# Gate and up of six ffn chunks as 2 by 2 blocks with seven block products, in a two-layer mixer network on one core

## The chip, the cores and the metric

The kernel runs on one core of one Trainium2 chip. TensorE multiplies, VectorE and ScalarE do the elementwise work, GpSimd and SyncE mostly issue transfers. The metric is the device time in microseconds, the median of the runs shown. Traces of profiled executions show where it goes.

## The reference

Each of two layers applies, to 256 tokens of width 1024, a SwiGLU ffn, a mixer, cross attention to 256 memory tokens, and a second ffn; a layer-norm stands behind each. All is float32.

```python
D_FF = 2816
def swiglu(x, w_gate, w_up, w_down):
    return (jax.nn.silu(x @ w_gate) * (x @ w_up)) @ w_down
...
    for l in range(DEPTH):
        h = layer_norm(ALPHA * h + 0.5 * swiglu(h, ffn1_gate[l], ffn1_up[l], ffn1_down[l]),
                       ln_g[l, 0], ln_b[l, 0])
        ...
        h = layer_norm(ALPHA * h + mix, ln_g[l, 1], ln_b[l, 1])
        h = layer_norm(ALPHA * h + cross_attn(h, mem, ca_q[l], ca_k[l], ca_v[l], ca_o[l]),
                       ln_g[l, 2], ln_b[l, 2])
        h = layer_norm(ALPHA * h + 0.5 * swiglu(h, ffn2_gate[l], ffn2_up[l], ffn2_down[l]),
                       ln_g[l, 3], ln_b[l, 3])
```

## The kernel before

The activations are two tiles `h[0]` and `h[1]` of 128 tokens x 1024. Every float32 product is made of three products of shorter numbers: an operand is split into a high half (`hi`, a cast on ScalarE) and a low half (`lo`, the value less its high half, on VectorE), and `mm_rows` adds hi x hi, hi x lo and lo x hi. `split` (lines 60 to 62) issues the cast (L61) and the subtraction (L62). Weights are split on the chip: `load` fetches 1 MB into a `raw` tile (three of them) and splits it in two pieces of 128x1024 into tiles `whi` and `wlo` (eight of each). A 128x512 product with 128 rows of the contraction is three matmuls.

An ffn (line 380) walks over its 2816 hidden columns in five chunks of 512 and one of 256. For a chunk, `all_products` multiplies the transposed activations `xTh`, `xTl` with gate and with up: 2 token tiles x 8 slices of the contraction x 3 = 48 matmuls each, 96 for both, into PSUM tiles `acc`. ScalarE takes silu of the gate product into `sg` (L406), VectorE multiplies it with up's (`gated`, L410). `turn` transposes the result: four transfers deal it to the tile `dealt`, VectorE's 32x32 block transpose writes `square` (L422), and a split makes `ah` and `al`. With these the rows of `down` are multiplied into four sums `dn` (`ys[i][m]`: token tile i, half m of the columns), which are kept over the whole ffn. The chunk's down products follow one chunk behind.

`finish` (line 292) closes an ffn and the other blocks: `tail` multiplies the last three down pieces, for h0's two sums and then h1's, and VectorE adds each sum to `h` (L320), takes its statistics (L322, L324), adds epsilon (L326), waits for GpSimd's power (L327), and normalises in two steps of two halves each (L330, L334). Then `h[0]` goes to the next block by eight transposes on TensorE (L170) or, behind an ffn1, by way of `deal`: a copy, four transfers, two block transposes on VectorE (L546). `h[1]` follows by TensorE when the next block calls `pend`.

Most of the program is ordered by a scheduler of the framework, which follows its own estimates of when operands are there. Stretches under `manual_schedule` keep the order in which they are written, for the engines named. Each engine runs its own instructions in order.

## Time and profile before

| | |
|---|---|
| runs, us | 1099.81, 1097.89, 1098.06; median 1098.06 |
| span of the profiled execution | 1094.9 us |
| TensorE, mean granted clock | 0.998 |
| TensorE matmuls, busy | 1079.6 us (99%) |
| VectorE, ScalarE, GpSimd busy | 836.3 us, 585.0 us, 61.0 us |
| transfers | 232.90 MB, mean 213 GB/s |

The profile gives no time of its own for the profiled execution but the span, from its first instruction to its last; the runs' median is 3.2 us above it. In the views, PE is TensorE, PEld its weight load, DVE VectorE, ACT ScalarE, POOL GpSimd, SP SyncE. L62 is line 62 of the kernel. A group's row gives its count, the busy time and the mean of one in ns, then the idle time of the engine ahead of it and what ended it. The busy time of neighbouring matmuls overlaps, so their pitch is read from the chain. Between engines the time of an ffn can be read in its stages: chunk after chunk TensorE takes 20.72 us for gate and up and 10.36 us for down.

### The profile page before, as it was taken

What the parts mean: (1) busy time and instruction counts of PE and PEld (TensorE: products, weight loads), DVE (VectorE), ACT (ScalarE), POOL (GpSimd) and SP (SyncE); (2) the same over time, 40 slices, a digit from 0 to 9 for tenths busy, and PEclk for the clock granted to TensorE, in tenths of its full rate; (3) what the DMA queues carried; (4) which work ended last, traced back from release to release, by engine and by line L of the source; (5) the groups of instructions that cost most, each with busy time, mean ns of one, the idle gap of its engine ahead of it and who ended that gap; (6) DMA issues with size and microseconds to landing.
All of it is one profiled execution on the core that took longest, in us unless ns stands there. A gap on an engine that the chain in (4) does not pass through costs nothing.

```text
span 1094.9 us, 15563 instructions
## 1 busy us (share of the span) xinstructions
PE 1079.6 (99%) x6035; PEld 952.6 (87%) x6035; DVE 836.3 (76%) x1075; ACT 585.0 (53%) x811; POOL 61.0 (6%) x113
## 2 busy tenths in 40 slices
PE   9999999999999999999999999999999999999997
PEld 7888888889898888888888888888898988888886
DVE  6679678898889877666687655798988888766665
...
GB/s 326 302 285 226 212 215 170 244 180 164 185 273 176 141 293 217 237 214 217 154 266 265 218 216 206 231 143 261 183 135 217 229 208 163 259 242 211 219 167 38
DMA packets 123818, 232.90 MB, mean 213 GB/s; under 512 B 6432, under 2 KB 46656, under 8 KB 118624
## 3 DMA queue, kind: packets, MB, share of 16 engines
...
HBM read 216.15 MB, written 1.05 MB: 198 GB/s over the span
## 4 chain that ended last, share of the span: by engine, by line
PE 90%; DVE 7%; ACT 2%; issue 1%; DMA 0%; DVEq 0%; ACTq 0%
PE acc L106 60%; PE dn L106 27%; DVE wlo L62 2%; PE acc L170 1%; DVE square L971 1%; PE dn L766 1%; ACT xT L61 0%; DVE qTl L62 0%; DVE h L334 0%; ACT whi L61 0%; DMA h<-in_x_dram 0%; DVE h L330 0%; PE dn L825 0%; DVE xT L62 0%; DVE st L322 0%
## 5 line engine op out<-in xcount | busy, mean ns | idle before, releaser
L62 DVE TENSOR_TENSOR wlo<-raw,whi 128x1024 fp32r<-128x1024 f32 (+1 forms) x396 | 474.1, 1213 | 181.4 <-ACT whi L61 170.6
L61 ACT CAST whi<-raw 128x1024 fp32r<-128x1024 f32 (+1 forms) x396 | 402.5, 1040 | 312.4 <-PE dn L106 117.3
L106 PE MATMUL acc<-whi,xT 128*128 128x512 f32 x1312 | 395.0, 380 | 0.0
L106 PEld LDWEIGHTS acc<-whi,xT 128*128 128x128 f32 x1312 | 247.8, 189 | 35.2
L106 PE MATMUL acc<-wlo,xT 128*128 128x512 f32 x656 | 248.6, 379 | 0.0
L106 PE MATMUL acc<-xT,whi 128*128 128x512 f32 x576 | 142.6, 382 | 4.0 <-DVE xT L62 4.0
L106 PEld LDWEIGHTS acc<-wlo,xT 128*128 128x128 f32 x656 | 124.0, 189 | 17.5
L106 PE MATMUL dn<-whi,ah 128*128 128x512 f32 x346 | 131.3, 379 | 0.0
L106 PE MATMUL dn<-wlo,ah 128*128 128x512 f32 x346 | 131.1, 379 | 0.0
L106 PE MATMUL dn<-whi,al 128*128 128x512 f32 x346 | 131.1, 379 | 0.0
L106 PEld LDWEIGHTS acc<-xT,whi 128*128 128x128 f32 x576 | 103.8, 190 | 16.3 <-ACT whi L61 4.6
L106 PE MATMUL dn<-whi,xT 128*128 128x512 f32 x288 | 88.8, 383 | 0.0
L106 PEld LDWEIGHTS acc<-xT,wlo 128*128 128x128 f32 x576 | 75.6, 191 | 4.3 <-DVE wlo L62 0.4
L106 PE MATMUL acc<-xT,wlo 128*128 128x256 f32 x576 | 76.4, 275 | 0.0
L106 PEld LDWEIGHTS dn<-wlo,ah 128*128 128x128 f32 x346 | 65.4, 189 | 9.3
L106 PEld LDWEIGHTS dn<-whi,al 128*128 128x128 f32 x346 | 65.4, 189 | 9.3
L106 PEld LDWEIGHTS dn<-whi,ah 128*128 128x128 f32 x346 | 65.4, 189 | 9.2
L422 DVE STREAM_TRANSPOSE square<-dealt 128x512 f32<-128x512 f32 x40 | 63.8, 1658 | 0.8 <-DMA dealt<-sg 0.7
L327 POOL TENSOR_TENSOR rs<-rs,nhalf 128x1 f32<-128x1 f32 x16 | 14.9, 929 | 867.3 <-DVE rs L326 859.8
L106 PEld LDWEIGHTS dn<-whi,xT 128*128 128x128 f32 x288 | 54.4, 190 | 8.5 <-DVE xT L62 1.1
L106 PE MATMUL dn<-wlo,xT 128*128 128x512 f32 x144 | 54.7, 380 | 0.0
L320 DVE SCALAR_TENSOR_TENSOR h<-h,dn 128x512 f32<-128x512 f32 x31 | 21.2, 684 | 31.4 <-PE dn L106 31.4
...
## 6 DMA issues: line engine op xcount, KB each, us to landing
raw<-in_ffn_up_dram SPq DMA_DIRECT2D x44, 1024.0 KB, 4.9
raw<-in_ffn_down_dram SPq DMA_DIRECT2D x44, 1024.0 KB, 5.1
raw<-in_ffn_gate_dram SPq DMA_DIRECT2D x42, 1024.0 KB, 5.0
raw<-in_w_in_dram SPq DMA_DIRECT2D x24, 1024.0 KB, 4.9
...
raw<-in_ca_k_dram SPq DMA_DIRECT2D x8, 1024.0 KB, 5.0
raw<-in_w_out_dram SPq DMA_DIRECT2D x8, 1024.0 KB, 4.7
raw<-in_ca_v_dram SPq DMA_DIRECT2D x8, 1024.0 KB, 4.9
```

The source lines that it names most:

```text
L61: nc.scalar.copy(hi, src)
L62: lows.append(nc.vector.tensor_tensor(lo, src, hi.bitcast(F32), op=ALU.subtract))
L106: nc.tensor.matmul(o, w, x, start=start, stop=stop)
L170: nc.tensor.transpose(pt[:, k, :], src[:, (4 * j + k) * P : (4 * j + k + 1) * P], unit)
L320: nc.vector.scalar_tensor_tensor(v, v, ALPHA / scale, sums(y[i][n]), op0=ALU.mult, op1=ALU.add)
L327: nc.gpsimd.tensor_tensor(rs, rs, nhalf[:, 0:1], op=ALU.pow)
L422: nc.vector.transpose(d.rearrange("p k (i b) -> p b k i", b=4), x[:, :, i, :].rearrange("p b (j k) -> p b k j", k=4))
L766: nc.tensor.matmul(o[g, hh, :], kc[:, hh, g], x, start=True, stop=True)
L971: nc.vector.transpose(pt.rearrange("p m (i r b) -> p b (m i) r", i=2, b=4), pr[hh])
```

## The change

In three of the four ffns (`BLOCKS`; all but layer 0's ffn1) chunks 1 and 3 are computed as 2 by 2 blocks. The token tiles are one pair; gate and up of 512 columns are another, and the two halves of the contraction the third. The four block products of gate and up take 8 multiplications; with sums and differences of the blocks 7 are enough. Each is 128 tokens x 512 rows x 512 columns: 12 matmuls. The activation blocks are combined by VectorE and ScalarE once for an ffn (`forms`, kept as halves in `kTh` and `kTl`), the weight blocks anew for each chunk: tile `ta` holds gate's upper rows, tile `tb` up's lower rows, in the place of the layer-norm's parameters. Three of the four weight sums are made by transfers from GpSimd's queue that add to what stands in the tile (`added`), the fourth by VectorE (`summed`). Each state of a tile is split before the next sum overwrites it. The products are combined by `plus`, `silu` and `times`.

Besides, every ffn is now a list of units (12 matmuls each, or a call), ordered by hand for TensorE, VectorE and ScalarE. `pump` fetches and splits the weights ahead of the units. A split piece is 128x2048, and four are kept (`WIDE`). The tail behind the units is in `finish`, outside the hand-made order. `turn` comes two units behind its chunk and reads the dealt tile in another order; each down piece of a full chunk is fetched by four transfers, 32 partitions each. The tokens of `h` are permuted by the matrices of the transposes (`pdn`), and `deal` of `h[0]` behind ffn1 is gone: it takes TensorE's transposes. The lines of the changed kernel that the rows below name: L74 and L75 are the cast and the subtraction of `split`, L123 is a matmul, L192 a transpose, L341 to L355 the layer-norm, L543 `joined`, L552 to L562 `forms`, L631 `plus`.

```diff
+BLOCKS = ((), (1, 3), (1, 3), (1, 3))
...
+    RAW = 3
+    WIDE = 4
...
+    def split_tiles(ncol):
+        h = wp.tile([P, 2048], F32R, tag="whi", name="whi", bufs=WIDE)
+        w = wp.tile([P, 2048], F32R, tag="wlo", name="wlo", bufs=WIDE)
...
-            for s in range(2):
-                h = wp.tile([P, 1024], F32R, tag="whi", name="whi", bufs=8)
-                w = wp.tile([P, 1024], F32R, tag="wlo", name="wlo", bufs=8)
-                h = h.rearrange("p (k c) -> p k c", c=ncol)
-                w = w.rearrange("p (k c) -> p k c", c=ncol)
-                r = raw[:, s * half : (s + 1) * half, :]
-                if fine:
-                    todo += [(h[:, b, :], w[:, b, :], r[:, b, :]) for b in range(half)]
-                else:
-                    split(h, w, r)
-                hi.append(h)
-                lo.append(w)
...
+                for b in range(0, step, step // 2):
+                    split(*(x[:, b : b + step // 2, :] for x in (h, w, raw)))
...
+        gb = wp.tile([P, 2, DM], F32, tag="gb", name="gb")
...
-            if deal and not i:
-                dealt = deal(h[0])
-        if deal:
-            dealt()
-        return lambda: transposed(h[1], 1, xTh, xTl, jdn if flip else idn)
-    def project_back(slabs, late, gb, scale, between=lambda: None):
+        return lambda: transposed(h[1], 1, xTh, xTl, units[1])
...
+            def turn(c, x):
+                ah, al = act_tiles()
+                for i in range(NT):
+                    d = fp.tile([P, 4, P], F32, tag="up", name="square")
+                    nc.vector.transpose(
+                        d.rearrange("p k (b r) -> p b k r", b=4), x[:, :, i, :].rearrange("p b (k j) -> p b k j", j=32)
+                    )
+                    split(ah[:, :, tok(i)], al[:, :, tok(i)], d)
+                acts[c] = ah, al
...
-                    nc.vector.transpose(
-                        d.rearrange("p k (i b) -> p b k i", b=4), x[:, :, i, :].rearrange("p b (j k) -> p b k j", k=4)
-                    )
-                    split(ah[:, :, tok(i)], al[:, :, tok(i)], d)
...
+                def prepare():
+                    p.hi, p.lo = split_tiles(p.ncol)
+                    if half:
+                        for b in range(2):
+                            g = slice(b * p.hi.shape[1] // 2, (b + 1) * p.hi.shape[1] // 2)
+                            split(p.hi[:, g, :], p.lo[:, g, :], p.raw[:, g, :])
+                    else:
+                        split(p.hi, p.lo, p.raw)
+                    then()
...
+                        src = down[c * CHUNK : (c + 1) * CHUNK].rearrange("(a k j) c -> a j k c", a=4, j=32)
+                        for a in range(4):
+                            loads.append(nc.sync.dma_start(
+                                raw[a * 32 : a * 32 + 32], src[a, :, 2 * u : 2 * u + 2, :]
+                            ))
...
+                            if i == 1:
+                                x = deal(state["s"])
+                                defer(lambda: turn(c, x), 2)
...
+            def joined(j):
+                f = tile4()
+                x, y = whole(0, j)
+                nc.vector.tensor_tensor(f, x.bitcast(F32), y.bitcast(F32), op=ALU.add)
+                return f
+            def forms(a11, a21, a22):
+                def put(n, f):
+                    split(*form(n), f)
+                z5 = tile4()
+                nc.scalar.copy(z5, a21)
+                s3 = tile4()
+                nc.vector.tensor_tensor(s3, a11, a21, op=ALU.subtract)
+                nc.vector.tensor_tensor(z5, a22, z5, op=ALU.subtract)
+                put(Z5, z5)
+                nc.vector.scalar_tensor_tensor(a11, z5, -1.0, a11, op0=ALU.mult, op1=ALU.subtract)
+                put(S3, s3)
+                put(S2, a11)
+                a12 = joined(1)
+                s4 = tile4()
+                nc.vector.scalar_tensor_tensor(s4, a11, -1.0, a12, op0=ALU.mult, op1=ALU.subtract)
+                put(S4, s4)
...
+                def added(name, m, k0):
+                    nc.gpsimd.dma_start(
+                        st[name],
+                        m[k0 * P : (k0 + 4) * P, c0 : c0 + CHUNK].rearrange("(k p) c -> p k c", p=P),
+                        accum_op=ALU.add,
+                    )
...
+                def summed():
+                    nc.vector.tensor_tensor(st["a"], st["a"], st["b"], op=ALU.add)
...
+                b11 = part("a", fetched("a", gate, 0, "ta"), lambda: added("a", up, 0), True)
+                b22 = part("b", fetched("b", up, 4, "gb"), lambda: added("b", up, 0))
+                b21 = rows_piece(gate, 4, c0)
+                ta = part("a", nothing, summed)
+                tb = part("b", nothing, nothing)
+                tc_ = part("a", nothing, lambda: added("a", gate, 4))
...
+                td = part("a", nothing, ended)
...
+                def silu(i, f, o):
+                    if "s" not in st:
+                        st["s"] = activations()
+                    v = halves(st["s"][:, i, :])
+                    plus(v, sums(f), sums(o))
+                    nc.scalar.activation(v, v, AF.Silu)
+                def times(i, f):
+                    v = halves(st["s"][:, i, :])
+                    nc.vector.scalar_tensor_tensor(v, sums(f), -1.0, v, op0=ALU.mult, op1=ALU.mult)
+                def p1():
+                    st["u"] = copied(product_of(whole(0, 0), b11))
+                def p2():
+                    silu(0, st["u"], product_of(whole(0, 1), b21))
+                def p5():
+                    st["v"] = copied(product_of(form(Z5), ta))
+                def p3():
+                    st["q"] = product_of(form(S4), b22)
+                def p6():
+                    o = product_of(form(S2), tc_)
+                    plus(st["u"], st["u"], o)
+                    f = snap()
+                    plus(f, st["u"], st["v"])
+                    plus(f, f, st["q"])
+                    times(0, f)
+                def p7():
+                    plus(st["u"], st["u"], product_of(form(S3), tb))
+                    plus(st["v"], st["v"], st["u"])
+                def p4():
+                    o = product_of(whole(1, 1), td)
+                    silu(1, st["u"], o)
+                    times(1, st["v"])
+                    x = deal(st["s"])
+                    defer(lambda: turn(c, x), 2)
+                return [
+                    ([b11], p1), ([b21], p2), ([ta], p5), ([b22], p3), ([tc_], p6), ([tb], p7), ([td], p4)
+                ]
...
+                def pump(free):
+                    nonlocal fetched, made, live, raws
+                    live -= free
+                    while True:
+                        while fetched < len(order) and (raws < RAW if order[fetched].ring else order[fetched].free()):
+                            order[fetched].fetch()
+                            raws += order[fetched].ring
+                            fetched += 1
+                        if made == len(order) or live == WIDE:
+                            return
+                        order[made].prepare()
+                        raws -= order[made].ring
+                        live += 1
+                        made += 1
+                pump(0)
+                for x, (ws, run) in enumerate(units):
+                    for f in [f for at, f in waiting if at <= now[0]]:
+                        f()
+                    waiting[:] = [(at, f) for at, f in waiting if at > now[0]]
+                    run()
+                    now[0] += 1
+                    pump(sum(final[w] == x for w in ws))
...
+                def second():
+                    a11 = joined(0)
+                    forms(a11, *pend())
+                return [
+                    g[0][0], g[1][0], p1, call(second), p2, g[0][1], g[1][1], *u[0], *u[1],
+                    p5, p3, p6, *g2[0], *downs[0][0], p7, *downs[0][1], p4,
+                    *g2[1], q1, *u2[0], *u2[1], q2,
+                    *downs[1][0], q5, q3, *downs[1][1], q6, *downs[2][0], q7, *downs[2][1], q4,
+                    *g4[0], *g4[1], *downs[3][0], *u4[0], *u4[1], *downs[3][1], *half,
+                ]
...
+            end = [down_piece(end_chunk - 1, 0), down_piece(end_chunk - 1, 1), down_piece(end_chunk, 0)]
+            with tc.manual_schedule(engines=ffn_engines):
+                run_units(sequence(), end)
```

The order of instructions shows the change in these places. First TensorE at the end of ffn2 in layer 0. The tiles dn_3852 to dn_3855 of before, and dn_3873 to dn_3876 of the change, are the sums of h0 (two) and h1 (two), and h0_72 is h0. Before:

```order
L106 MATMUL dn_3854<-wlo_4903,ah_4738 128x512
L106 MATMUL dn_3854<-whi_4902,al_4739 128x512
L106 MATMUL dn_3855<-whi_4878,ah_4655 128x512
L106 MATMUL dn_3855<-wlo_4879,ah_4655 128x512
L106 MATMUL dn_3855<-whi_4878,al_4656 128x512
L106 MATMUL dn_3855<-whi_4882,ah_4655 128x512
L106 MATMUL dn_3855<-wlo_4883,ah_4655 128x512
L106 MATMUL dn_3855<-whi_4882,al_4656 128x512
L170 MATMUL acc_4983<-idn_77,h0_72 128x128 x4
L170 MATMUL acc_4990<-idn_77,h0_72 128x128 x4
L106 MATMUL dn_3855<-whi_4888,ah_4655 128x512
L106 MATMUL dn_3855<-wlo_4889,ah_4655 128x512
```

And of the change:

```order
L123 MATMUL dn_3874<-whi_4654,al_4697 128x512
L123 MATMUL dn_3875<-whi_4654,al_4697 128x512
L123 MATMUL dn_3875<-whi_4654,ah_4696 128x512
L123 MATMUL dn_3875<-wlo_4655,ah_4696 128x512
L123 MATMUL dn_3875<-whi_4654,al_4697 128x512
L123 MATMUL dn_3876<-whi_4654,al_4697 128x512
L123 MATMUL dn_3876<-whi_4654,ah_4696 128x512
L123 MATMUL dn_3876<-wlo_4655,ah_4696 128x512
L123 MATMUL dn_3876<-whi_4654,al_4697 128x512
L192 MATMUL acc_4779<-pdn_82,h0_72 128x128 x4
L192 MATMUL acc_4786<-pdn_82,h0_72 128x128 x4
L123 MATMUL dn_4855<-whi_4830,xT_89 128x512
```

Before, h0's transposes stand inside the last sum of h1, whose first 6 of 18 matmuls in the tail are ahead of them; of the change they stand behind the last matmul on all four sums, and the next ffn's first product on xT (dn_4855) follows.

VectorE at the same place (st and mv are the layer-norm's statistics, xT the transposed activations, wlo the low halves of the next ffn's weights), before:

```order
L330 SCALAR_TENSOR_TENSOR h0_72<-h0_72,mv_4947,lng_4016 128x512 x2
L334 SCALAR_TENSOR_TENSOR h0_72<-h0_72,rs_4949,lnb_4017 128x512 x2
L320 SCALAR_TENSOR_TENSOR h1_73<-h1_73,dn_3854 128x512
L322 BN_STATS st_4956<-h1_73 128x6
L62 TENSOR_TENSOR wlo_5038<-raw_5035,whi_5037 128x1024
L62 TENSOR_TENSOR wlo_5042<-raw_5035,whi_5041 128x1024
L62 TENSOR_TENSOR xT_87<-acc_4983,xT_87 128x4x128
L62 TENSOR_TENSOR xT_87<-acc_4990,xT_87 128x4x128
L320 SCALAR_TENSOR_TENSOR h1_73<-h1_73,dn_3855 128x512
L62 TENSOR_TENSOR wlo_5048<-raw_5045,whi_5047 128x1024
L322 BN_STATS st_4956<-h1_73 128x6
```

And of the change:

```order
L341 SCALAR_TENSOR_TENSOR h1_73<-h1_73,dn_3876 128x512
L347 TENSOR_SCALAR rs_4745<-mv_4743 128x1
L351 SCALAR_TENSOR_TENSOR h0_72<-h0_72,mv_4743,gb_4283 128x512 x2
L355 SCALAR_TENSOR_TENSOR h0_72<-h0_72,rs_4745,gb_4283 128x512 x2
L343 BN_STATS st_4752<-h1_73 128x6
L345 BN_AGGR mv_4807<-st_4752 128x2
L347 TENSOR_SCALAR rs_4809<-mv_4807 128x1
L351 SCALAR_TENSOR_TENSOR h1_73<-h1_73,mv_4807,gb_4283 128x512 x2
L355 SCALAR_TENSOR_TENSOR h1_73<-h1_73,rs_4809,gb_4283 128x512
L75 TENSOR_TENSOR xT_89<-acc_4779,xT_89 128x4x128
L75 TENSOR_TENSOR xT_89<-acc_4786,xT_89 128x4x128
L355 SCALAR_TENSOR_TENSOR h1_73<-h1_73,rs_4809,gb_4283 128x512
```

The halves of xT stood ahead of h1's last sum, and now stand behind its layer-norm but for one piece.

VectorE in the opening of ffn2, layer 0, from h1's xT halves on (acc_3608 and acc_3615 are the transposes of h1, kTl and kTh hold the forms, wlo_3657 is the low half of up's second piece). Before, where acc_3758 and acc_3765 are those transposes:

```order
L62 TENSOR_TENSOR xT_87<-acc_3758,xT_87 128x4x128
L62 TENSOR_TENSOR xT_87<-acc_3765,xT_87 128x4x128
L410 TENSOR_TENSOR sg_3678<-acc_3745,sg_3678 128x512
L62 TENSOR_TENSOR wlo_3860<-raw_3857,whi_3859 128x1024
L62 TENSOR_TENSOR wlo_3864<-raw_3857,whi_3863 128x1024
L62 TENSOR_TENSOR wlo_3870<-raw_3867,whi_3869 128x1024
L62 TENSOR_TENSOR wlo_3874<-raw_3867,whi_3873 128x1024
```

And of the change:

```order
L75 TENSOR_TENSOR xT_89<-acc_3615,xT_89 128x4x128
L554 TENSOR_TENSOR snap_3624<-snap_3606,acc_3608 128x512
L555 TENSOR_TENSOR snap_3622<-acc_3615,snap_3622 128x512
L75 TENSOR_TENSOR kTl_92<-snap_3622,kTh_91 128x512
L557 SCALAR_TENSOR_TENSOR snap_3606<-snap_3622,snap_3606 128x512
L75 TENSOR_TENSOR kTl_92<-snap_3624,kTh_91 128x512
L75 TENSOR_TENSOR kTl_92<-snap_3606,kTh_91 128x512
L543 TENSOR_TENSOR snap_3634<-xT_89 128x512
L562 SCALAR_TENSOR_TENSOR snap_3636<-snap_3606,snap_3634 128x512
L75 TENSOR_TENSOR kTl_92<-snap_3636,kTh_91 128x512
L631 TENSOR_TENSOR sg_3653<-snap_3595,acc_3640 128x512
L75 TENSOR_TENSOR wlo_3657<-raw_3540,whi_3656 128x2048
```

Nine steps on forms and the sum of one product (L631) now stand between h1's halves and the next weight split.

483 lines of the change are left out of this document (302 added, 181 removed).

## The prediction

> **What bounds the kernel now.** I read the page's busy table and its chain of waits first. Columns: busy time, share of the span, instructions; then the chain's share by engine.
>
> ```profile
> span 1094.9 us, 15563 instructions
> PE 1079.6 (99%) x6035; PEld 952.6 (87%) x6035; DVE 836.3 (76%) x1075; ACT 585.0 (53%) x811; POOL 61.0 (6%) x113
> PE 90%; DVE 7%; ACT 2%; issue 1%; DMA 0%; DVEq 0%; ACTq 0%
> ```
>
> TensorE is the bound: it is idle for some 15 of 1094.9 us, and 7 of these lie behind the last matmul. So fewer matmuls are worth their full time, as long as nothing else comes late. Then two windows by stage (span, then busy time of PE, PEld, DVE, ACT, POOL, the granted clock, DMA share, GB/s): the attention's end with the start of ffn2 in layer 0, and that ffn2's body.
>
> ```profile
> 282.00:420.00 138.00, 137.13 (x725) 121.48 (x724) 115.17 (x154) 72.75 (x104) 3.71 (x4) 1.00 0.63 217
> 420.00:557.00 137.00, 137.00 (x659) 120.29 (x658) 95.08 (x101) 64.05 (x74) 1.84 (x2) 1.00 0.64 209
> ```
>
> In the ffn VectorE has 42 of 137 us free and TensorE waits for nobody. That is the room which the change spends.
>
> **The matmuls that go.** Chain rows (start, length, count) give the price:
>
> ```profile
> 422.89 20.72 PE acc L106 x96
> 443.61 10.36 PE dn L106 x48
> ```
>
> 20.72 / 96 = 0.2158 us for a 128x512 matmul. A block chunk issues 7 x 12 = 84 in place of 96; six chunks save 72, **-15.5 us**. A unit of 12 takes 2.59 us.
>
> **The end of each ffn.** The chain's row for h0's transposes, and the layer-norm's rows from before's end of ffn2, layer 0 (a timeline: start, length; in brackets the idle time before and who ended it):
>
> ```profile
> 544.74 0.87 PE acc L170 x8
> 539.60 0.69 DVE L320 SCALAR_TENSOR_TENSOR h<-h,dn 128x512 f32<-128x512 f32 x1 [2.46 <-PE dn L106]
> 540.32 0.69 DVE L322 BATCH_NORM_STATS2 st<-h 128x6 f32<-128x512 f32 x1
> 541.05 0.21 DVE L324 BATCH_NORM_AGGREGATE mv<-st 128x2 f32<-128x12 f32 x1
> 541.29 0.15 DVE L326 TENSOR_SCALAR rs<-mv 128x1 f32<-128x1 f32 x1
> 541.36 1.40 DVE L330 SCALAR_TENSOR_TENSOR h<-h,mv,lng 128x512 f32<-128x512 f32 x2
> 542.68 1.41 DVE L334 SCALAR_TENSOR_TENSOR h<-h,rs,lnb 128x512 f32<-128x512 f32 x2
> 544.01 0.68 DVE L320 SCALAR_TENSOR_TENSOR h<-h,dn 128x512 f32<-128x512 f32 x1
> 547.59 1.29 DVE L62 TENSOR_TENSOR xT<-acc,xT 128x512 fp32r<-128x512 f32 x2
> ```
>
> Before, h0's two sums were complete 36 matmuls (7.8 us) ahead of the end, and its layer-norm ran under h1's matmuls. The order of the change shows the four sums completing together: at this place 12, 8, 4 and 0 matmuls before the end (2.6, 1.7, 0.9 and 0 us), with h0's transposes after the last. I count from the last matmul. VectorE takes h0's sum at -2.6, its statistics, h0's and h1's next sums and two statistics by +1.7 (six steps of 0.72), the aggregate and h1's last sum by 2.7, rs, L351 and L355 twice by 5.4. By its queue it then ends h1's layer-norm too, but for one piece, before the first low half of xT: 0.7 + 0.3 + 1.3 + 0.7 + 0.65 more, **9.1 us**. TensorE fills 0.9 of it with transposes (which before had too) and 0.4 with two matmuls: 7.8 lost. And the last down piece needs the half chunk's ah and al. ScalarE casts the next ffn's second gate piece (1.9, below) ahead of ah, VectorE splits it (2.27) ahead of al, and its tiles come free only 6 matmuls (1.3 us) before ah is needed: 1.9 + 0.6 - 1.3 = 1.2, and 0.6 more for al. **+9.6** here.
>
> The same count at the other ends. Layer 0's ffn1: h0's sums complete 22 and 17 matmuls early; sum, sum, two statistics, h1's sum, aggregate, a 1.22 split, rs and two pairs end at +3.4, the transposes (0.9) come on top of before, and the mixer's wait below shrinks by 1: **+3.3**. Layer 1's ffn1: 15 and 11 early, h0 normalised at +5.7, transposes 0.9, ah and al 1.4, less 2.0 for that wait, which this cover ends: **+6.0**.
>
> ```profile
> 733.69 1.75 PE L106 MATMUL acc<-xT,whi 128*128 128x512 f32 x7 [2.01 <-DVE xT L62]
> 1087.24 0.28 PE L106 MATMUL acc<-whi,al 128*128 128x256 f32 x1
> 1087.56 0.42 DVE L314 TENSOR_TENSOR h<-h,acc 128x256 f32<-128x256 f32 x1 [1.12 <-PE acc L106]
> 1090.16 1.53 DVE L334 SCALAR_TENSOR_TENSOR h<-h,rs,lnb 128x512 f32<-128x512 f32 x3
> ```
>
> The last end: before, VectorE is done 4.2 us after the last matmul (1090.16 + 1.53 - 1087.52). Now h0's sums come 3.5 and 2.6 us ahead of it, so that all of h0's layer-norm (ended at +3.6) stands before h1's remaining four statistics, its last sum and its own norm, at 9.0: **+4.8**.
>
> **The weights in one piece, and the forms.** Means from the groups by form (count, then busy us, mean ns):
>
> ```profile
> L62 DVE TENSOR_TENSOR wlo<-raw,whi 128x1024 fp32r<-128x1024 f32 x388 | 468.8, 1223 | 181.4 <-ACT whi L61 170.6 <-PE acc L106 7.8
> L62 DVE TENSOR_TENSOR wlo<-raw,whi 128x512 fp32r<-128x512 f32 x8 | 5.3, 701 | 0.0
> L61 ACT CAST whi<-raw 128x1024 fp32r<-128x1024 f32 x388 | 398.0, 1049 | 312.4 <-PE dn L106 117.3 <-PE acc L106 110.9 <-DVE square L422 22.7
> L61 ACT CAST whi<-raw 128x512 fp32r<-128x512 f32 x8 | 4.6, 622 | 0.0
> L422 DVE STREAM_TRANSPOSE square<-dealt 128x512 f32<-128x512 f32 x40 | 63.8, 1658 | 0.8 <-DMA dealt<-sg 0.7
> L546 DVE STREAM_TRANSPOSE square<-dealt 128x512 f32<-128x512 f32 x4 | 2.6, 687 | 0.0
> L410 DVE TENSOR_TENSOR sg<-acc,sg 128x512 f32<-128x512 f32 x40 | 26.0, 685 | 3.6 <-PE acc L106 3.2
> L62 DVE TENSOR_TENSOR xT<-acc,xT 128x512 fp32r<-128x512 f32 x36 | 23.5, 687 | 5.8 <-ACT xT L61 5.8
> L406 ACT ACTIVATE sg<-acc 128x512 f32<-128x512 f32 x38 | 22.1, 596 | 15.0 <-PE acc L106 14.9
> ```
>
> 512 elements cost 0.52 us more on VectorE and 0.43 on ScalarE, so I estimate 2048 at 1.22 + 2 x 0.52 = 2.27 and 1.05 + 2 x 0.43 = 1.90. Work hardly changes (two of 1024 are 2.4); what changes is that a low half now follows its cast after 4.2 us, where halves overlapped, and that nothing small gets between. The turning copy reads in the order in which L546 read, so I take 0.69 for 1.66: about 39 us of VectorE go, in ffn bodies where it was not waited for.
>
> Opening of a block ffn, by the queues (second and third pair of rows above, from ffn2 of layer 0). Before:
>
> ```profile
> 375.22 7.77 PE acc L106 x36
> 382.99 1.05 PE acc L170 x8
> ```
>
> 36 matmuls covered h1's layer-norm exactly. Now 36 do so again, but two splits of 2.27 stand in it for three of 1.15: from xT's first half to h1 ready is 10.2 us where it was 8.6, **1.65** late. xT's own low halves come behind a split of 2.27 that awaits a 1.90 cast: some **1.0** for h0 and 0.5 for h1. Then the forms. From h1 normalised, VectorE: a split 2.3, `joined` 3.0, xT's halves 4.3, two forms 5.7, ScalarE's cast and the low half 7.0, S2 7.7, two low halves 9.1, `joined` and S4 10.5, cast and low half 11.8, the plus of p2 12.5; silu 13.1 and only then the cast of up's second piece, 15.0, and its split, **17.3**. TensorE meanwhile: transposes, p2, two units on gate, two on up, the first held until xT's half at 3.6: it asks at 14.0 and can go two matmuls further. **3.0** late. Opening: 6.2 us; 5.2 in layer 1's ffn1, whose first wait is in the 9.6 above.
>
> From there to q4's start TensorE has 33 units, 85.4 us. VectorE has about 25 splits (56.8), two sums (4.5), four gatings, 17 block operations and twelve instructions of turning at 0.69 (22.8): 84 us. The lead of four pieces was spent in the opening, so VectorE runs without slack, and every wait of its own goes on to TensorE: it waits for a product ahead of each group of L631, with the next split behind it. Four places show this in the order: the second half of chunk 0's down, q2's weights, chunk 1's down behind p4's silu, and q6 behind a turn. I walked them at 1.1, 0.9, 2.3 and 2.0: **6.3 in each ffn**; without them, nothing. So 12.5 + 11.5 + 12.5 = **+36.5**, between 9 (half of the opening's waits hidden, none inside) and 48 (four more waits each at 1).
>
> **The adding transfers** have no row. The nearest:
>
> ```profile
> raw<-in_ffn_up_dram SPq DMA_DIRECT2D x44, 1024.0 KB, 4.9
> m<-in_mem_dram POOLq DMA_DIRECT2D x32, 32.0 KB, 6.5
> ```
>
> Below: 4.9 us, as 1 MB from SP. Above: 4.9 + 6.5 = 11.4, POOL's start-up added to the bytes. ta has about 12 us (from b11's split to its next cast, behind the forms), tb 9 to 10 (three splits, two gatings, a turn). I take 6.5 to 9: hidden, 0; at 11.4, tb costs 2 in six chunks, +12. They bring no bytes that a plain load did not bring before, and at the window's DMA share of 0.64 there is room. The Trainium skill ("Collectives: The Full Stack", Part 3, on why ReduceScatter is half of AllGather) says that an add in the transfer reads two sources and ran 1.93 times slower than a copy; no trace here shows one. By it the transfer would be an estimated 9.5 us, at the edge of tb's cover, and the sum would stay.
>
> On POOL the adding transfer stands ahead of the norm's power, whose input VectorE makes later still: 0. Down pieces as four transfers, one tile for the norm's parameters, the mixer's h0 without its dealing: hidden under PE, 0.
>
> **Sum**, against the profiled span: -15.5 + 3.3 + 9.6 + 6.0 + 4.8 + 36.5 = +44.7, 1139.6. The shown median is 1098.06, 3.2 above the span, so **1143**.
>
> **Rivals.** (a) *The queues stay ahead*: the scheduler's four-piece lead hides opening and inner waits, and the ends cost a third, as the 39 us of turning freed suggest. Against: the order puts both layer-norms in front of xT whatever the lead. The one thing that decides is whether the waits together stay under 15.5 us; with 0 inside and 8 at the ends it is -7.5, 1090. 0.10. (b) *Only the ends count*: +23.7 - 15.5 and 9 inside, 1115; 0.20. (c) *TensorE comes back slow.* At the start it did:
>
> ```profile
> 6.99 0.85 PE dn L441 x2
> ```
>
> 0.43 each where 0.216 is usual, after idling. There are three waits over 3 us at the ends; eight matmuls at double time after each add 5: 1148. With tb late as well (+12), 1160 and above; 0.15. The Trainium skill ("TensorE: Matmul & The Clock Gate", Part 1) puts the fall to half clock behind one idle window of about 3.4 us; the trace before holds no such wait past its start, so it neither bears it out nor speaks against it. That the change does not do what it says is out: the order has 4262 for 4334 wide matmuls.
>
> **Chances.** Forecast 0.55, (b) 0.20, (c) 0.15, (a) 0.10. Range 1107 to 1165: all of the forecast's bounds but the last few us, (b), most of (c). A measurement here tells 0.2% (2 us) from no change: faster 0.08, same 0.02, slower 0.90.
>
> **What would show it.** PE idle of 8 before the first product on xT in layer 1's ffn1, released by DVE xT; 3 and 6 before h0's transposes at the ffn1 ends; a last matmul 11 to 12 us ahead of the span's end; waits of 2 to 3 on wlo at up's second piece; splits at 2.27. Wrong if VectorE shows under 90% in the block windows, or those waits under 1.

## The result, and the profile after

The changed kernel takes 1248.7 us (median of four runs, 1244.69 to 1250.4), beside 1097.98 us for the kernel before (four runs, 1097.89 to 1099.81): a ratio of 1.1365, with a 95% interval of 1.1343 to 1.1387. The forecast of a slower kernel held; the forecast of 1143, and its range up to 1165, did not. The profiled execution took 1244.69 us, with a span of 1242.9.

The page of the changed kernel, its span, busy table and granted clock first, then rows of its groups and its transfers (engine, shape and count; for a group the busy time, the mean of one in ns and the idle time ahead with its releaser; for a transfer the KB and the median us from issue to landing):

```profile
span 1242.9 us, 15451 instructions
PE 1111.9 (89%) x5979; PEld 958.7 (77%) x5979; DVE 892.0 (72%) x1040; ACT 607.1 (49%) x724; POOL 85.2 (7%) x131
PEclk9998999999999988999989898999999999998998
L75 DVE TENSOR_TENSOR wlo<-raw,whi 128x2048 fp32r<-128x2048 f32 x110 | 251.1, 2290 | 99.9 <-ACT whi L74 99.9
L435 DVE STREAM_TRANSPOSE square<-dealt 128x512 f32<-128x512 f32 x40 | 28.2, 707 | 111.3 <-DMA dealt<-sg 111.3
L74 ACT CAST whi<-ta 128x2048 fp32r<-128x2048 f32 x24 | 45.6, 1902 | 69.0 <-DMA ta<-in_ffn_gate_dram 60.4
ta<-in_ffn_up_dram POOLq DMA_DIRECT2D x6, 1024.0 KB, 11.4
tb<-in_ffn_up_dram POOLq DMA_DIRECT2D x6, 1024.0 KB, 8.9
ta<-in_ffn_gate_dram POOLq DMA_DIRECT2D x6, 1024.0 KB, 11.4
dealt<-sg SPq DMA_DIRECT2D x80, 128.0 KB, 7.1
```

TensorE is busy for 32.3 us more than before (1111.9 for 1079.6), although it issues fewer matmuls, and not busy for 131.0 us in place of 15.3 (span less busy time): 32.3 + 115.7 are the 148.0 us by which the span grew. VectorE waits 111.3 us for the dealt tile, where it waited 0.7 us before (one transfer of a deal then took 3.2 us to land, now 7.1), and ScalarE 60.4 us for `ta`, the tile that transfers add to. The block transpose itself is as cheap as forecast, 0.707 us.

The two windows by stage that answer to those of before, from the attention's end into ffn2 of layer 0 and the rest of that ffn (span, then busy time of PE, PEld, DVE, ACT, POOL, the granted clock, DMA share, GB/s):

```profile
282.00:430.00 148.00, 141.58 (x759) 124.62 (x758) 127.26 (x170) 82.13 (x116) 6.32 (x7) 1.00 0.59 187
430.00:600.00 170.00, 142.82 (x635) 121.50 (x635) 107.34 (x82) 71.82 (x58) 5.72 (x5) 0.93 0.80 205
```

In the second, TensorE is busy for 143 of 170 us, at a clock of 0.93, and VectorE for 107. Neither is the bound here: both wait.

One place shows how these hang together: chunk 0's turn in ffn2 of layer 0. In the kernel before, by the timelines of SP's queue and of VectorE (start, length, engine, operation; in brackets the idle time before and its releaser):

```profile
444.63 2.60 SPq L419 DMA_DIRECT2D dealt<-sg  x4
451.05 1.64 DVE L422 STREAM_TRANSPOSE square<-dealt 128x512 f32<-128x512 f32 x1
```

And in the changed kernel, by the same views with those of GpSimd and of TensorE:

```profile
429.37 1.31 POOL L583 DMA_DIRECT2D tb<-in_ffn_up_dram  x1 [26.62 <-DVE wlo L75]
431.56 1.26 POOL L583 DMA_DIRECT2D ta<-in_ffn_gate_dram  x1 [0.89 <-DVE wlo L75]
432.53 3.63 SPq L428 DMA_DIRECT2D dealt<-sg  x4
446.69 0.71 DVE L435 STREAM_TRANSPOSE square<-dealt 128x512 f32<-128x512 f32 x1 [9.83 <-DMA dealt<-sg]
448.11 0.79 PE L123 MATMUL dn<-whi,ah 128*128 128x512 f32 x1 [7.54 <-ACT ah L74]
```

Before, the turn came 6.4 us behind its deal's first issue and found the tile there. Now it heads VectorE's queue about 4 us behind the issue, and the tile lands only 14.2 us behind it. For 9.83 us VectorE does nothing, and the splits and sums queued behind the turn wait with it. TensorE waits 7.54 us for `ah`.

The turn of chunk 1 in the same ffn shows the second way in which a late turn reaches TensorE. ScalarE's next cast of weights stands in its queue behind the casts of the turn, and TensorE waits for these weights:

```profile
488.03 0.71 DVE L435 STREAM_TRANSPOSE square<-dealt 128x512 f32<-128x512 f32 x1 [9.11 <-DMA dealt<-sg]
491.78 1.89 ACT L74 CAST whi<-raw 128x2048 fp32r<-128x2048 f32 x1
493.72 0.80 PE L123 MATMUL acc<-whi,xT 128*128 128x512 f32 x1 [8.37 <-ACT whi L74]
```

Each of the three block ffns has one such wait: 8.37, 7.54 and 7.56 us.

The deal of 0.5 MB of chunk 0 is slow because two adding transfers of 1 MB were issued just ahead of it, as the run without them shows below. The queues in the window from 430 to 450 us (packets, MB, share of the 16 transfer engines) of the changed kernel:

```profile
q0 software_dynamic: 1056, 2.10, 60.4%
q1 hardware_dynamic: 2073, 2.51, 41.0%
```

The engines are full for nearly the whole window. The adding transfers take 60.4% of it for 2.10 MB, the plain ones 41.0% for 2.51 MB: 28.8 and 16.3 points for a MB, so an added byte holds the engines 1.8 times as long as a plain one here.

Last, what a wait does to TensorE's clock. Windows of 2 us around the wait of 4.49 us at 553.90 (span of the window, busy time and count of matmuls, granted clock, share of the transfer engines, GB/s):

```profile
552.00:554.00 2.00, 0.10 (x1) 1.00 0.85 300
554.00:556.00 2.00, 2.00 (x5) 0.51 0.01 4
556.00:558.00 2.00, 2.00 (x7) 0.64 0.00 0
558.00:560.00 2.00, 2.00 (x11) 1.00 0.00 0
```

Behind the wait 5 and 7 matmuls run in two windows where 11 is usual. The first 24 matmuls behind the wait of 5.47 us at 1182.21 take 7.05 us by the chain, where 24 x 0.2158 is 5.18: 1.9 us, which no row of idle time shows.

```profile
1182.21 7.05 PE dn L123 x24
```

### The profile page after: what moved, and what is told of

It reads as the page before. It is cut to its first block, busy times and chain, and to the rows that moved or that the text cites. A ratio compares the mean times of both kernels' runs of the same rounds, so it can differ in the third digit from the quotient of the medians.

```text
span 1242.9 us, 15451 instructions
## 1 busy us (share of the span) xinstructions
PE 1111.9 (89%) x5979; PEld 958.7 (77%) x5979; DVE 892.0 (72%) x1040; ACT 607.1 (49%) x724; POOL 85.2 (7%) x131
## 5 line engine op out<-in xcount | busy, mean ns | idle before, releaser
L75 DVE TENSOR_TENSOR wlo<-raw,whi 128x1024 fp32r<-128x1024 f32 (+2 forms) x250 | 415.5, 1676 | 118.4 <-ACT whi L74 114.7
L74 ACT CAST whi<-raw 128x1024 fp32r<-128x1024 f32 (+2 forms) x250 | 347.0, 1412 | 137.0 <-PE dn L123 54.1
L123 PE MATMUL acc<-whi,xT 128*128 128x512 f32 x880 | 273.9, 387 | 24.2 <-ACT whi L74 23.5
L123 PEld LDWEIGHTS acc<-whi,xT 128*128 128x128 f32 x880 | 169.5, 193 | 51.3 <-ACT whi L74 24.7
L123 PE MATMUL acc<-wlo,xT 128*128 128x512 f32 x440 | 170.5, 388 | 7.5 <-DVE wlo L75 7.4
L123 PE MATMUL dn<-whi,ah 128*128 128x512 f32 x346 | 137.3, 401 | 40.7 <-ACT ah L74 35.5
L123 PE MATMUL dn<-whi,xT 128*128 128x512 f32 x480 | 151.6, 391 | 10.1 <-DVE xT L75 6.9
L123 PE MATMUL dn<-wlo,ah 128*128 128x512 f32 x346 | 137.6, 399 | 8.6 <-DVE wlo L75 8.6
L123 PE MATMUL acc<-xT,whi 128*128 128x512 f32 x576 | 142.5, 382 | 0.4 <-DVE xT L75 0.4
L123 PE MATMUL dn<-whi,al 128*128 128x512 f32 x346 | 135.3, 395 | 0.4 <-DVE al L75 0.4
L74 ACT CAST ah<-square 128x512 fp32r<-128x512 f32 x40 | 24.7, 619 | 204.0 <-DVE square L435 204.0
L123 PEld LDWEIGHTS dn<-whi,xT 128*128 128x128 f32 x480 | 92.4, 194 | 28.6 <-DVE xT L75 11.2
L123 PEld LDWEIGHTS acc<-xT,whi 128*128 128x128 f32 x576 | 103.9, 190 | 12.8 <-DVE xT L75 1.2
L123 PEld LDWEIGHTS dn<-whi,ah 128*128 128x128 f32 x346 | 69.3, 200 | 55.0 <-ACT ah L74 39.0
L435 DVE STREAM_TRANSPOSE square<-dealt 128x512 f32<-128x512 f32 x40 | 28.2, 707 | 111.3 <-DMA dealt<-sg 111.3
L123 PEld LDWEIGHTS acc<-wlo,xT 128*128 128x128 f32 x440 | 84.6, 192 | 22.7 <-DVE wlo L75 10.9
L123 PE MATMUL dn<-wlo,xT 128*128 128x512 f32 x240 | 93.6, 390 | 5.5 <-DVE wlo L75 5.5
L123 PEld LDWEIGHTS dn<-wlo,ah 128*128 128x128 f32 x346 | 69.2, 200 | 21.5 <-DVE wlo L75 11.3
L74 ACT CAST whi<-ta 128x2048 fp32r<-128x2048 f32 x24 | 45.6, 1902 | 69.0 <-DMA ta<-in_ffn_gate_dram 60.4
L123 PEld LDWEIGHTS acc<-xT,wlo 128*128 128x128 f32 x576 | 75.6, 191 | 4.3 <-DVE wlo L75 0.4
L123 PEld LDWEIGHTS dn<-whi,al 128*128 128x128 f32 x346 | 68.7, 199 | 12.5 <-DVE al L75 2.5
L123 PE MATMUL acc<-xT,wlo 128*128 128x256 f32 x576 | 76.2, 275 | 0.0
```

What stands on the lines that cost most here:

```text
L74: nc.scalar.copy(hi, src)
L75: lows.append(nc.vector.tensor_tensor(lo, src, hi.bitcast(F32), op=ALU.subtract))
L123: nc.tensor.matmul(o, w, x, start=start, stop=stop)
L435: nc.vector.transpose(d.rearrange("p k (b r) -> p b k r", b=4), x[:, :, i, :].rearrange("p b (k j) -> p b k j", j=32))
```

## The experiments

The changed kernel is the starting point of each diff, unless it says otherwise. Times are in us, of one execution each, and medians of two for the last three kernels; the kernel before took 1096.6 to 1098 beside them.

**Units alone, without blocks** (BLOCKS empty): 1146.8.

```diff
-BLOCKS = ((), (1, 3), (1, 3), (1, 3))
+BLOCKS = ((), (), (), ())
```

> No chunk is computed as blocks (the list of block chunks is empty for all four ffns); the units queued by hand, the wide splits and the moved turns stay. All 4334 matmuls of before are back. Theory 'blocks': the adding transfers and the block work cost most of the 150 us; the hand-made queue alone costs the ends of the ffns (about 24) and a few waits: 1115 to 1140. Rival 'queue': turns two units behind their chunk and whole 2048 splits are what costs, blocks or not: 1180 or more.

It came out between the two: all that the change does besides the blocks costs 49, and the blocks on top of it 102, in spite of their 15.5 us of saved matmuls. In this kernel no transfer adds, and VectorE waits for the dealt tile all the same (the view of waits: who waits for whom, us, times, longest):

```profile
DVE square L435 <- DMA dealt<-sg: 127.9, 20, 9.0
```

The deals are late here behind plain loads. One deal of the kernel before, with the load issued ahead of it, the landing of the deal's transfers and the share of the transfer engines from its issue on (timeline, transfers, window):

```profile
471.94 0.37 SPq L76 DMA_DIRECT2D raw<-in_ffn_up_dram  x1
475.67 2.61 SPq L419 DMA_DIRECT2D dealt<-sg  x4
dealt<-sg SPq DMA_DIRECT2D x4, 128.0 KB, 3.1
475.70:480.90 5.20, 5.20 (x26) 4.56 (x25) 2.43 (x2) 2.12 (x3) 0.00 (x0) 1.00 0.77 201
```

And one of the units without blocks, where two loads stand ahead of it:

```profile
499.03 2.60 SPq L91 DMA_DIRECT2D raw<-in_ffn_up_dram  x2
502.47 2.64 SPq L428 DMA_DIRECT2D dealt<-sg  x4
dealt<-sg SPq DMA_DIRECT2D x4, 128.0 KB, 8.0
502.50:512.50 10.00, 10.00 (x48) 8.74 (x47) 2.14 (x1) 0.00 (x0) 0.00 (x0) 1.00 1.09 282
```

From a deal's first issue to its last landing the traces have 5.5 us before, 9.1 in the changed kernel and 9.4 here (medians over all deals). At 15 of the 22 deals before, the nearest load was issued 2.7 to 3.8 us ahead; at all 20 deals here, 1.2 us or less. So the hand-made order also puts loads closer ahead of the deals. That this is what delays them is read from the traces; no run moved the loads.

**The adding transfers left out**: 1202.4.

```diff
-b11 = part("a", fetched("a", gate, 0, "ta"), lambda: added("a", up, 0), True)
+b11 = part("a", fetched("a", gate, 0, "ta"), nothing, True)
...
-tc_ = part("a", nothing, lambda: added("a", gate, 4))
+tc_ = part("a", nothing, nothing)
```

> The 18 adding transfers are left out (the weight blocks stay unsummed but for VectorE's sum, so the block products take other numbers); all else as changed. Theory 'adding transfers fill the DMA engines': the dealt transfers fall from 7.1 to under 5 us, the waits of PE on ah (35 us) to under 12, the waits of ScalarE on ta (60 us) go, the clock rises to 0.98: 1150 to 1180. Rival 'four-part down loads and SyncE's order': the dealt transfers stay at 6 us or more and the span above 1215.

Between the expectations again: 46 us come back, so the transfers were not hidden, and 104 stay. A deal's transfer lands in 5.8 us in place of 7.1, and VectorE's waits for it fall from 111.3 to 73.3. At the place shown above, chunk 0 in ffn2 of layer 0, no load stands ahead of the deal now. The turn starts 6.2 us behind the first issue in place of 14.2, VectorE waits 1.87 us in place of 9.83, and TensorE waits for no `ah` there:

```profile
433.21 2.63 SPq L428 DMA_DIRECT2D dealt<-sg  x4
439.41 0.71 DVE L435 STREAM_TRANSPOSE square<-dealt 128x512 f32<-128x512 f32 x1 [1.87 <-DMA dealt<-sg]
```

**The turn four units behind its chunk, in place of two** (in plain and in block chunks): 1186.2.

```diff
-defer(lambda: turn(c, x), 2)
+defer(lambda: turn(c, x), 4)
```

> A turn comes four units behind its chunk in place of two (10.4 us in place of 5.2); nothing else changes. Theory 'the turn at the head of VectorE's queue': VectorE's waits on dealt fall from 111 us to under 40, the splits behind it come in time, PE's waits on ah and on the casts behind it shrink by 30 or more: 1185 to 1215. Rival 'late whatever the queue': the transfer's delay is only met elsewhere, 1235 or more.

This one number gives back 62 us. VectorE's waits for the dealt tile fall to a fifth, while nothing in the transfers is changed:

```profile
DVE square L435 <- DMA dealt<-sg: 22.8, 8, 4.4
PE dn L123 <- ACT ah L74: 34.9, 6, 8.5
```

The largest sum that stays is six waits of TensorE for `ah`. With the adding transfers left out as well:

> The adding transfers are left out, as before in these experiments, and a turn comes four units behind its chunk. Theory 'both act by the same wait' (the deal that the turn awaits): the two gains of 44 and 60 overlap, 1150 to 1175. Rival 'two independent costs': they add up, 1135 to 1148.

It took 1173.4. The two gains overlap: with the turn at four units the adds cost 13, with the turn at two 46. Most of what the adding transfers cost was paid through the turn, which stood at the head of VectorE's queue while the deal crept in behind them.

**Turn at four units, without blocks**: 1135.4.

> No chunk as blocks, and a turn four units behind its chunk. Theory 'turn too early': VectorE's 128 us of waits on dealt go below 30 and with them the waits on splits in the chunks; what is left are the ends: 1110 to 1122. Rival 'wide splits': the waits of 1.84 on wlo stay, 1135 or more.

From 1146.8 only 11 came back. The time is the rival's, but the waits of 1.84 that it named are gone but for one: what is left are mostly waits at the ends of the ffns, four of 3.2 to 5.8 us, and slower matmuls, at a clock of 0.983.

**One transfer for each down piece** (and the turn's reading order of before), with blocks and without: 1239.9 and 1142.8.

```diff
-src = down[c * CHUNK : (c + 1) * CHUNK].rearrange("(a k j) c -> a j k c", a=4, j=32)
-for a in range(4):
-    loads.append(nc.sync.dma_start(raw[a * 32 : a * 32 + 32], src[a, :, 2 * u : 2 * u + 2, :]))
+src = down[c * CHUNK : (c + 1) * CHUNK].rearrange("(p k) c -> p k c", p=P)
+loads.append(nc.sync.dma_start(raw, src[:, 2 * u : 2 * u + 2, :]))
```

> With blocks, as changed, but each down piece of a full chunk is fetched by one transfer again (128 partitions, as before the change) and the block transpose reads the dealt tile in before's order; its cost goes back from 0.7 to about 1.7 us, 40 times. Theory 'the four-part loads hold up the deals': dealt falls from 7.1 to under 5 us, VectorE's wait on dealt from 111 to under 70, the span by 20 or more, 1215 or less, in spite of the dearer transposes. Rival 'adding transfers alone': dealt stays at 6.5 or more, 1240 to 1285.

> No chunk as blocks, and each down piece in one transfer with before's reading order. Theory 'the four-part loads hold up the deals': dealt falls from 7.5 to 4 us or less, the span to 1115 to 1130. Rival 'the deals are late because they are issued behind whole weight loads on SyncE's queue': dealt stays at 6 or more, 1140 or more.

5 us below the lowest of the changed kernel's four runs, which spread over 5.7, and 4 below the units alone. The deal's transfers land in 6.6 and 6.3 us, in place of 7.1 and 7.5, and a block transpose takes 1.34 and 1.54 us again. So the four-part loads, and the issues on SP's queue that they add, are not the main cause; a few us of theirs may be hidden behind the slower transposes.

**The deals from GpSimd's queue**, without blocks: 1193.7, 47 us more than from SP's.

```diff
-nc.sync.dma_start(x[a * 32 : a * 32 + 32], s[:, :, a * P : (a + 1) * P])
+nc.gpsimd.dma_start(x[a * 32 : a * 32 + 32], s[:, :, a * P : (a + 1) * P])
```

> Units without blocks, turns two behind, and the deals issued from GpSimd's queue in place of SyncE's. Theory 'first in, first out': the deals are slow as they stand behind the weight loads on SyncE's queue, so from another queue they land in 4.5 us or less. Rival 'shared engines': 6 us or more, as before on SyncE (7.5), and VectorE's wait on dealt stays over 110.

The deal's transfers land no sooner from here, in 7.6 us. What GpSimd's queue itself adds is in this figure, so that the run shows no gain by this way, and leaves open how much the place in SP's queue cost.

**The tail in the written order on TensorE**, as it stands, and without blocks and with the turn at four: 1264.2 and 1139.0.

```diff
+with tc.manual_schedule(engines={E.PE}):
     return finish(tail, ys, 0.5, held["gb"], last=last, units=(idn, jdn) if name == "ffn1" else (pdn, pdn))
```

> The last three down pieces and the transposes of h0 are put in their written order on TensorE (h0's two sums first, then h1's), in all four ffns; nothing else changes. Theory 'completing together': the waits of 4.1 and 4.5 us on h before the transposes, the two on xT behind them and part of the 12 us behind the last matmul go: 10 to 18 us less, 1225 to 1233. Rival 'the half chunk is late': the written order meets ah and al of the half chunk after 12 matmuls and waits there for as much: within 4 us of the changed kernel.

> As units with turns four behind (no blocks), and the last three down pieces with h0's transposes in their written order on TensorE. Here the half chunk is followed by 24 matmuls of chunk 3's down, so that its ah should be there. Theory 'completing together': the waits of 3.2 before the transposes and the slow clock behind each go: 1112 to 1124. Rival 'the half chunk is late here too': 1133 or more.

Some 16 us worse, and 3.5, which is within the 5.7 by which the changed kernel's own runs differ. With h0's sums closed first, TensorE comes to the half chunk's product in the block ffns while its `ah` is not there, and waits 8.9, 7.8 and 6.4 us. Without blocks it waits for the split of the last weights instead. The scheduler's mixed order of the four sums, which I had counted as the loss, was the better one with these waits about.

**Down products later** (in chunks 0 and 3, the half chunk earlier; turn at four, tail as written), with the adding transfers and without: 1214.6 and 1186.5.

```diff
-p5, p3, p6, *g2[0], *downs[0][0], p7, *downs[0][1], p4,
-*g2[1], q1, *u2[0], *u2[1], q2,
+p5, p3, p6, *g2[0], p7, *g2[1], *downs[0][0], p4, *downs[0][1],
+q1, *u2[0], *u2[1], q2,
...
-*g4[0], *g4[1], *downs[3][0], *u4[0], *u4[1], *downs[3][1], *half,
+*g4[0], *g4[1], *u4[0], *u4[1], *downs[3][0], *half, *downs[3][1],
```

> With blocks. Turns four units behind; chunk 0's down comes three units later, behind the seventh product, chunk 3's down behind all of chunk 4's up, the half chunk ahead of chunk 3's second down piece; the tail in written order. Theory 'what is left of the block cost are turns that come right ahead of their down': the waits on ah (35 us with turns at four) fall under 10, the clock to 0.985: 1140 to 1165. Rival 'VectorE has no room': the waits move to wlo and whi, 1175 or more.

> The same, and the adding transfers left out. Theory 'the adding transfers cost by themselves': 12 to 25 less than with them, since tb and ta are awaited by ScalarE. Rival 'once the turns have room the adding transfers hide': within 5 of it.

Worse than with the turn at four alone (1186.2): the waits for `ah` halved, to 16.8 us, and others for weights came in their place. Part of this may be the tail, which cost by itself in the run before; the two were not tried apart. Without the adding transfers 28 us come back, more than the 12 to 25 of the first expectation.

**Splits in two halves of 1024**, with the turn at four, with blocks and without: 1164.3 and 1126.1.

```diff
-def piece(fetch, then=lambda: None, half=False):
+def piece(fetch, then=lambda: None, half=True):
...
-split(w.hi, w.lo, st[name])
+for b in range(2):
+    g = slice(2 * b, 2 * b + 2)
+    split(w.hi[:, g, :], w.lo[:, g, :], st[name][:, g, :])
```

> With blocks and turns four behind (1186), every weight piece split in two halves of 128x1024 again, one behind the other. Theory 'the wide split': a late piece costs 1.84 for its whole subtraction and 0.8 with halves, at some 12 places with the slow clock behind them: 1166 to 1178. Rival 'VectorE has no room': two halves cost 2.44 in place of 2.29, 1184 to 1195.

> Units without blocks, turns four behind (1135), splits in two halves. Theory 'the wide split' here too: the ends of the ffns and the last ffn wait less, 1118 to 1130. Rival 'order alone': 1133 or more.

22 and 9 us less, the first 2 us below its expected range, the second inside it. TensorE's waits of 1.84 us on a piece's low half, which stood at seven places of the changed kernel, are gone; one of 2.19 is left. Without blocks, what is left is almost only at the ends of the ffns: three waits of 3.38 us ahead of h0's transposes, and 5.00 in the last ffn.

**The sums by GpSimd from plain loads** (blocks, turn at four): 1233.3.

```diff
-nc.gpsimd.dma_start(
-    st[name],
-    m[k0 * P : (k0 + 4) * P, c0 : c0 + CHUNK].rearrange("(k p) c -> p k c", p=P),
-    accum_op=ALU.add,
-)
+w.raw = raw_tile(CHUNK)
+rows_in(w.raw, m, k0 * P, c0)
...
+nc.gpsimd.tensor_tensor(st[name], st[name], w.raw, op=ALU.add)
```

> With blocks and turns four behind (1186); the three sums that the adding transfers made are made by GpSimd from plainly loaded weights (three more pieces through the raw ring for a chunk). Theory 'an adding transfer takes its engines' time twice': dealt falls to 5.5 us as without the sums, tb and ta come in time, 1168 to 1180, near the 1173 without the transfers. Rival 'GpSimd's sums are as late': over 9 us for one, 1186 or more.

47 us worse than by adding transfers. GpSimd takes 5.2 us for a sum for which VectorE took 2.29, and three more pieces for a chunk go through the ring of `raw` tiles; the two were not tried apart:

```profile
L589 POOL TENSOR_TENSOR ta<-ta,raw 128x2048 f32<-128x2048 f32 x12 | 62.6, 5220 | 130.1 <-DVE wlo L76 130.1
L607 DVE TENSOR_TENSOR ta<-ta,tb 128x2048 f32<-128x2048 f32 x6 | 13.8, 2292 | 0.2
```

**The waits filled with matmuls that nobody reads**: 1260.9.

```diff
+if blocks and u == i == 0 and c in (0, 3):
+    o = acc()
+    for _ in range(33 if c == 0 else 20):
+        nc.tensor.matmul(o, xTh[:, 0, tok(0)], xTh[:, 0:2, :], start=True, stop=True)
```

> The changed kernel with matmuls that nobody reads (33 ahead of chunk 0's first down unit, 20 ahead of chunk 3's, in the three block ffns), in the windows where TensorE waits for ah 7.5 and 4.5 to 5.9 us. 33 x 0.216 = 7.1 us and 20 x 0.216 = 4.3 us, so that hardly any idle time is left in these six windows and the matmuls themselves cost next to nothing. If the idle windows are what lowers the granted clock, it stays at 1.00 behind these six places, and the dearest 24 matmuls behind each no longer take 1.9 us more: about 11 us less than the changed kernel, 1233 to 1240, mean clock from 0.959 to 0.965 or above. If the clock falls for another reason (the mean load, the time of the run), the time stays at 1245 to 1252 and the clock behind these places still reads 0.5 to 0.6.

The time went the other way, for a reason that I had not seen: ahead of chunk 0's down the filler needed a PSUM bank, which a sum of VectorE behind the late turn had still to read, so it waited there itself, 38.4 us at three places. Ahead of chunk 3's down it ran through the wait, and this answers whether idle time lowers the clock. The windows there, the filler's last matmul at 558.7 and the first down product at 560.23, with an idle time of 1.17 us between:

```profile
560.00:562.00 2.00, 1.74 (x7) 1.00 0.02 8
562.00:564.00 2.00, 2.00 (x11) 1.00 0.00 0
564.00:566.00 2.00, 2.00 (x11) 1.00 0.00 0
566.00:568.00 2.00, 2.00 (x11) 1.00 0.25 47
```

The clock stays at 1.00 where the same place of the changed kernel read 0.51 and 0.64. The windows behind the other two filled places of this kind, from 784 and from 1197 us, read 1.00 too. So it was the idle time that lowered it. At the one in the last ffn, 22 matmuls behind the first two take 5.02 us, where 22 x 0.2158 is 4.75. This run shows the cause of the lower clock, and no way to a gain.

**The turn at three units with halves, then chunk 0's down products a block product later and chunk 3's two units later**: 1182.7 and 1170.8.

```diff
-defer(lambda: turn(c, x), 4)
+defer(lambda: turn(c, x), 3)
...
-p5, p3, p6, *g2[0], *downs[0][0], p7, *downs[0][1], p4,
+p5, p3, p6, *g2[0], p7, *downs[0][0], *downs[0][1], p4,
...
-*g4[0], *g4[1], *downs[3][0], *u4[0], *u4[1], *downs[3][1], *half,
+*g4[0], *g4[1], *u4[0], *downs[3][0], *u4[1], *downs[3][1], *half,
```

> Turns three units behind the deal in place of four, splits in two halves. In the version with four, the waits for ah at six places (45 us in all) are the only large ones left; there the turn stands behind p6's four sums and a split that came late, so it starts 14 us behind the deal's first issue although a deal lands in 7 to 8. If the turn's place in VectorE's queue is what is left, one unit earlier takes about 3 us from each: 1140 to 1152. If three units are too few for the deal to land (7.8 us from the last up unit, less the 4 that the issues take), VectorE waits for dealt again and the splits behind it come late: 1165 to 1185.

> As the run with turns at three units and halves, and chunk 0's down a block product later, chunk 3's two units later, so that ah has 2.6 and 5.2 us more. If the waits for ah are only the distance from the deal to the down product, they fall by these amounts more: 1120 to 1140, the best of the block versions, and still above the kernel before. If they are VectorE's and the transfers' throughput, the wait moves on to tb's or the next weights' split: within 5 us of that run.

At three units the rival holds: VectorE waits 61.5 us for the dealt tile where it waited 28.1 at four, and 18 us are lost. With the down products later as well, 12 us of it come back, which is between the two expectations. The waits for `ah` shrink from 43.8 to 9.2 us, but a new one stands at p7, which the later order puts ahead of the down products:

```profile
435.13 0.76 PE L123 MATMUL acc<-whi,kTh 128*128 128x512 f32 x1 [11.70 <-DVE snap L633]
```

Three of these come to 34.5 us: p7 wants the bank that p6's sums on VectorE have not yet read. The wait moved rather than went.

No version beats the kernel before. The best with blocks takes 1164, the best without 1126.

## Why the prediction was right in its sign and wrong in its size

The terms of the prediction beside what the profile of the changed kernel has for them. Idle times are sums of TensorE's rows of idle time at these places; the ends are taken by the working on record.

| term | predicted, us | measured, us |
|---|---|---|
| matmuls that go | -15.5 | -15.5 by the count of matmuls |
| the four ends | +23.7 | +16.9 |
| opening of the three block ffns | +17.6 | +16.0 |
| inside the three block ffns | +18.9 | +72.3 |
| inside layer 0's ffn1 | 0 | +11.5 |
| the rest of TensorE's busy time: slower matmuls, and ends of matmuls ahead of waits | 0 | about +46 |
| sum | +44.7 | about +147, of 148.0 |

The 46 are what is left of TensorE's busy time: 32.3 more, with 15.5 less by the matmuls that went and 1.7 more by h0's transposes. They are not all slower matmuls. Where a matmul of 128x512 follows another without idle time, the starts in the trace lie 42.8 us further apart in all than 0.2158 each, and 8.6 before: 34 us by a lower clock. The other 11 or 12 are the waits' own: the last matmul ahead of a wait counts as busy for 0.38 us and more, where the next one otherwise starts 0.216 behind it.

**The ends** were right in kind and somewhat large. The four places, by the working on record: 1.1, 6.9, 4.7 and 4.2 us, where 3.3, 9.6, 6.0 and 4.8 stood. Instead of one wait of 8 ahead of the first product on xT in layer 1's ffn1, the wait is split, the largest part ahead of h0's transposes (timelines of TensorE at the two ends in question):

```profile
608.86 1.94 PE L192 MATMUL acc<-pdn,h 128*128 128x128 f32 x8 [4.10 <-DVE h L355]
826.45 1.75 PE L192 MATMUL acc<-idn,h 128*128 128x128 f32 x8 [4.46 <-DVE h L355]
```

The last matmul stands 11.6 us ahead of the span's end, as forecast.

**The openings** were right: 5.5, 5.0 and 5.5 us, for 6.2, 5.2 and 6.2. The splits of 2048 took 2.29 us (2.27 forecast), the casts 1.90, the transposes 0.71 (0.69). A wait of 1.84 stands on `wlo` where up's second piece is due, a little under the 2 to 3 named.

**Inside the block ffns the step failed**, the one that put 6.3 us into each: "I walked them at 1.1, 0.9, 2.3 and 2.0". Of the 72.3 us, 33 are six waits for `ah`, 23.5 are the three for weights whose cast stood behind a late turn, and 15 are for low halves. The walk took VectorE's queue with the turn priced as "twelve instructions of turning at 0.69" and nothing for the four transfers that the first of them waits for. The trace of before had what was needed: SP's row of a deal, 2.60 us for the issues alone, and the turn 6.4 us behind their start. The change allows two units, 5.2 us, less what VectorE's `gated` and the issue take of it.

The place alone would have cost little: had the deals landed some 5.2 us behind their first issue, as in the row of before at 475.67, VectorE would have waited an estimated 1 us at each of the 20 turns (5.2 less the 4.3 at which the turn heads its queue), not 5.6 (111.3 over 20). The rest is what is in flight when a deal is issued.

That VectorE would have 84 us of work in 85.4 was beside the point. It was less busy than forecast (127.3 of 148 us, 86%, up to 430 us, and 107.3 of 170, 63%, behind, in the windows above). Of its 62.7 idle us in the second window, it spent 28.3 in front of a tile that had not landed, and 25.6 in front of ScalarE's casts of weights, part of them behind a turn. The walk left out one wait more: inside a turn each low half waits for ScalarE's cast of the same half (0.2 us in all before), by the view of waits

```profile
DVE al L75 <- ACT ah L74: 27.4, 40, 0.7
```

By the mark on record, "wrong if VectorE shows under 90% in the block windows", the account of why TensorE would wait was wrong. Moving the turn by two units gave back 62 us: that is the experiment which shows it. Layer 0's ffn1, which has no blocks, got nothing inside in the sum, and no reason for it. It waits 11.5 us there for weights, of which the turn at four units leaves 1.6.

**The adding transfers** were put at 6.5 to 9 us and "hidden, 0". Their medians are 8.9 (`tb`) and 11.4 (`ta`), the upper bound on record, and were not hidden: leaving them out gave 46 us. Little of that is ScalarE's own wait for them. Of its 60.4 us in front of `ta`, 41.0 at four places are for the plain load that fills the tile, as here,

```profile
461.57 0.37 SPq L91 DMA_DIRECT2D ta<-in_ffn_gate_dram  x1
466.97 1.90 ACT L74 CAST whi<-ta 128x2048 fp32r<-128x2048 f32 x1 [9.69 <-DMA ta<-in_ffn_gate_dram]
```

and 19.4 at three for an adding transfer; without the adding transfers 35.4 stay. For `tb`, of which the prediction feared 2 us in six chunks, it does not wait. Most of the 46 is paid by the deals that share the transfer engines with them, which the argument from "the window's DMA share of 0.64" did not see: the share is a mean over 137 us, and the deal is due in 5. The Trainium skill ("Collectives: The Full Stack", Part 3) had spoken against that argument: it has ReduceScatter, whose transfers add, 1.93 times slower than AllGather, whose transfers copy. The 1.8 times as much engine time per byte in the window above is near it. The estimate of 9.5 us that the prediction worked out from it lies between the two measured medians.

**The clock** was only in rival (c), at +5 for three long waits, and cost some 34. It fell behind many more waits than three, those for `ah` above all, which the prediction did not have. The filler shows that idle time is the cause. The Trainium skill ("TensorE: Matmul & The Clock Gate", Part 1) has half clock behind one idle window of about 3.4 us: the wait of 4.49 with 0.51 behind it agrees, as does the filled place, which stays at 1.00. The runs here show falls behind shorter waits too, as the last section tells. That the 34 us come about in this way is worked out from the starts of the matmuls, not tried place by place.

The rivals (a) and (b), with waits that stay below 15.5 us or stand at the ends alone, are out. Rival (c) had the clock right, at 1148 or 1160 and above; it took its waits from the ends and from a late `tb`, where most of them came from the deals. Turns and wide splits together are also 21 of the 49 us that the units cost without any block (1146.8 to 1126.1).

**What stays open.** In the best version with blocks six waits for `ah`, 45.0 us, remain. At chunk 0, three of them, the turn stands behind p6's sums and behind a split whose cast had waited for an adding transfer; at chunk 3 VectorE still waits for the dealt tile. Earlier turns met a tile that had not landed, later down products met a PSUM bank not yet read. An order that avoids all three was not found. Nor was it tried what moving the loads away from the deals gives.
